# A stream encoder of two layers: one memory block a round, a later norm transposition, and engine times by intervals in the scheduling guard

## The chip, the cores and the metric

The kernel runs on one core of a Trainium2 chip. The metric is the device time of one launch in microseconds; less is better. A time is the median of several runs; the profile is of one execution of its own.

## The reference

Two layers work on x (256 rows of 2048) and on a memory of 256 rows. Each layer adds a mixer (HGRN2, retention and Mamba2 heads side by side), an attention to the memory, and a gated FFN with a short convolution. Cut to what the change touches:

```
for l in range(DEPTH):                                       # DEPTH = 2
    x = x + hybrid_mixer(rmsnorm(x, norm_mix[l]), ...)       # 11 projections of h; three recurrences; w_out
    x = x + memory_cross_attention(rmsnorm(x, norm_xattn[l]),
                                   rmsnorm(mem, norm_mem[l]), wq, wkv, wo)
    x = x + conv_glu_ffn(rmsnorm(x, norm_ffn[l]), ...)       # silu(gate) * up, 5632 wide
return rmsnorm(x, norm_final)

def rmsnorm(x, w):  return x * rsqrt(mean(x * x, -1) + EPS) * w
def hybrid_mixer(...):
    proj = h @ w_in                   # split into hq hf hi hg | rq rk rv rg | z xbc dt
    hg_out  = grouped_rmsnorm(o_hg, hg_norm, 4)  * sigmoid(hg)
    ret_out = grouped_rmsnorm(o_r, ret_norm, 4)  * silu(rg)
    ssm_out = grouped_rmsnorm(y * silu(z), ssm_norm, 4)
    return concatenate([hg_out, ret_out, ssm_out]) @ w_out
def memory_cross_attention(h, mem_n, wq, wkv, wo):
    q = h @ wq;  k, v = split(mem_n @ wkv)
    return softmax(q k^T / sqrt(128)) v @ wo    # 4 heads
```

## The kernel before, in words

Everything is float32. For the matrix products each operand is split into a high part and a low part (what the high part leaves over), and three products of the parts are added up in PSUM.

**The stream.** All weights pass through PE in one fixed order, one *step* at a time; there are 895 steps, most with eight tiles of 128 columns, that is 16 matmuls. Step n uses the weight buffers wh_n and wl_n. `split_w_hi` writes `wh` on ACT from the loaded `raw`, three steps ahead; `split_w_lo` writes `wl` on DVE (raw minus wh), two steps ahead. There are five `wh`, four `wl` and five `raw`. In layer 0 the steps are, by this number: hf to 11, hq 12 to 19, hd (hi and the Mamba2 time step DT) 20 to 27, hg 28 to 35, xbc 36 to 67, z 68 to 83, rv 84 to 91, rq, rk and rg to 115, the output projection in two halves of the rows 116 to 131 and 132 to 147, then for the attention q 148 to 155, k 156 to 163, v 164 to 171, wo 172 to 179, then the FFN to 449. Layer 1 repeats this from 450 on.

**Side work.** Whatever is not a step (evacuations, norms, the recurrences, the split of the memory) is written as a Python generator that yields after a small piece; one piece is a *round*. After each step the loop calls `advance(False)`, which gives each generator a round. Those marked `first` (evacuations) always get it; the others only while the modelled backlog of DVE and that of ACT are at most BACKLOG. The backlog is what `Metered` counts for the instructions so far, by a rate and a fixed part for each, less the length of the steps (`step_done`). So the order of the instructions is set when the program is written out, and PE, DVE and ACT then run their lists in that order.

When a step needs something that is not yet in the lists (`need`), or a projection bank while all five are taken (`pj`), all generators are advanced, whatever the backlog, until it is there. Such a burst of DVE and ACT instructions then stands right ahead of the matmul that waits for it:

```
def advance(all_of_them=True):
    for e in list(gens):
        g, first = e
        if not (first or all_of_them) and (late["dve"] + dve.us > BACKLOG or late["act"] + act.us > BACKLOG):
            continue
        ...
def step_done(us):
    for k, e in (("dve", dve), ("act", act)):
        late[k] = max(0.0, late[k] + e.us - us)
```

**The parts that the change and the prediction touch.**

- `gen_rstd` turns a sum of squares into 1/rms: a sum over partitions on PE with ONES, Ln and Exp on ACT, and one Newton step on DVE (`newton`: two operations into `w`, one into the result). For the mixer it also turns the result R into a column form RC by small matmuls with CON (line 463), and ACT copies RC. The evacuations of hd (`hi<-pj,RC`, `DT<-pj,RC`) need RC and free the banks of hd. For the memory it does the same for RM and RMC.
- The HGRN tail: OG and SQ, two sums over heads (lines 425, 426), `VV`, Ln, Exp, Newton step, `pr` (the scaled result), a copy to `mo` on ACT, and its low part `mo<-pr,mo` on DVE. `mo` is the input of the output projection. The evacuations of the last z tiles stand behind the end of this tail.
- Mamba2's and retention's group norms (`gen_ssm_norm`, `gen_ret`) end the same way, in `pr` and `mo`; the second half of the output projection (from step 132) starts with the `mo` of the second half of the Mamba2 heads.
- `gen_res` adds the output projection to X and forms H for q (`H<-X`, `ACC<-ACC,sq`).
- `gen_mem` loads the memory in eight pairs of blocks into `ya` (two buffers, `ya<-memT` on SP), and makes `mh` for each of the 16 blocks: the high part on ACT, in layer 0 also the square on ACT, the low part `mh<-ya,PAR,mh` on DVE and, in layer 0, the sum `RM<-RM,sq`. A block takes two rounds. It starts when the pages under `mh` are free, which are those of four `mo`. Step 156 is the first that reads `mh`; it reads blocks 0 to 7, and step 157 blocks 8 to 15.

Of the kernel before, what the change touches and what calls it, by code (L numbers as in the profile page):

```python
# [11 lines left out]
P = 128  # L12
T = 256
# [115 lines left out]

GROUP_MAX = 1056  # L130
NWARM = 4
BACKLOG = 10.0


def group_steps(plan):
# [112 lines left out]
class Metered:  # L248


    def __init__(self, engine, rate, fixed, fast=()):
        self.engine, self.rate, self.fixed, self.fast, self.us = engine, rate, fixed, fast, 0.0

    def __getattr__(self, name):
        f = getattr(self.engine, name)
        if name == "preload_act_table_set":
            def g(*a):
                self.us += 1.28
                return f(*a)
            return g  # L260

        def g(out, *a, **k):
            n = 1
            for d in out.shape[1:]:
                n *= d
            self.us += (n / (2 if name in self.fast else 1) + self.fixed) / self.rate
            return f(out, *a, **k)  # L267
        return g


def build(tc, ws, xT, memT, par, con, masks, rot, dec, outT):
    nc = tc.nc
    act, dve, pe, gp = Metered(nc.scalar, 1200.0, 190), Metered(nc.vector, 960.0, 64, ("tensor_scalar",)), nc.tensor, nc.gpsimd

    pc = tc.alloc_tile_pool(name="const", bufs=1)
    pw = tc.alloc_tile_pool(name="weights", bufs=1)
# [31 lines left out]
    def pcol(l, key, i, n=1):  # L308
        return parcol(l * PLAYER + PCOL[key] + i, n)
# [54 lines left out]
    def wait(*keys):  # L364
        while any(k not in flags for k in keys):
            yield
# [23 lines left out]
    def fn(out, src, f, **kw):  # L390

        want = "natural_log_exp_and_others" if f in (AF.Exp, AF.Ln) else "silu_and_others" if f in (AF.Silu, AF.Tanh) else table[0]
        if want != table[0]:
            act.preload_act_table_set(want)
            table[0] = want
        act.activation(out, src, f, **kw)
# [31 lines left out]
    def gen_rstd(acc_key, acc, out, outc, key):  # L428
        yield from wait(acc_key)
        yield  # L430
        while lock.get("v"):
            yield
        lock["v"] = 1
        yield from take(1)
        if rest:
            ps = bank()
            for i, t in enumerate([acc] + rest):
                pe.matmul(ps[:, :T], ones, t, start=i == 0, stop=i == len(rest))  # L438
        else:
            while lock.get("sq", 0) == 2:  # L440
                yield
            lock["sq"] = lock.get("sq", 0) + 1
            hl = tmp("v", [P, T], F32R, bufs=1), tmp("sq", [P, T], F32R, bufs=2)
            split_ones(acc, *hl)
            yield
            yield
            ps = bank()
            sum_ones(ps[:, :T], *hl)
            lock["sq"] -= 1
        yield  # L450
        v = tmp("v", [P, T], bufs=1)
        dve.tensor_scalar(v, ps[:, :T], 1.0 / D, EPS, ALU.mult, ALU.add)
        give()
        yield
        yield from newton(v, out)
        lock["v"] = 0
        flags.add(key)
        if outc is not None:
            yield
            yield from take(1)  # L460
            ps = bank()
            for i in range(2):
                pe.matmul(ps[:, i:i + 1], out[:, i * P:(i + 1) * P], ident[:, 0:1], start=True, stop=True)
            yield
            act.copy(outc, ps[:, 0:2])
            give()
            flags.add(key + ("c",))
# [85 lines left out]
    def layer(l):  # L553
# [479 lines left out]
        def gen_ret(p):  # L1033
# [42 lines left out]

            OG, SQ, VV = q[:, b0:b0 + 2, :], k[:, b0:b0 + 2, :], A0[:, b0:b0 + 2, :]
            yield from gen_o(pg["rv"], lambda a: ((0, A0[:, a, :], 0, True, False), (1, A1[:, a, :], P, False, True)), lambda ps: fn(SQ, ps, AF.Square), lambda ps: act.copy(OG, ps), p)
            yield from gen_gstd(SQ, P, VV, SQ)
            G = pg["rg"]  # L1080
            for i in range(2):
# [10 lines left out]

        MH = {}

        MHP = [2, 3, 6, 10, 12, 13, 14, 15]

        def gen_mem():

            yield from wait((A, "mo", 5), (A, "mo", 7), (A, "mo", 13), (A, "mo", 15))
            raw = {}  # L1100

            def fetch(p):
                if p < KD // 2:
                    raw[p] = tmp("ya", [P, 2, T])
                    nc.sync.dma_start(raw[p], memT[:, 2 * p:2 * p + 2, :])
            fetch(0)
            fetch(1)
            for _ in range(4):
                yield
            for p in range(KD // 2):  # L1110
                t = page(MHP[p], [P, 2, 2 * T], F32R, "mh")
                for b in range(2):
                    kt = 2 * p + b
                    MH[kt] = t[:, b, :]
                    split_hl(MH[kt], raw[p][:, b, :], pcol(l, "norm_mem", kt))
                    if l == 0:
                        while lock.get("sq", 0) == 2:
                            yield
                        lock["sq"] = lock.get("sq", 0) + 1
                        sq = RM if kt == 0 else tmp("sq", [P, T], bufs=2)  # L1120
                        fn(sq, raw[p][:, b, :], AF.Square)
                    yield
                    split_lo(MH[kt], raw[p][:, b, :], pcol(l, "norm_mem", kt))
                    if l == 0:
                        if kt:
                            tt(RM, RM, sq, ALU.add)
                        lock["sq"] -= 1
                    flags.add((C, "m", kt))
                    yield
                fetch(p + 2)  # L1130
            flags.add("accm")

        def qk_evac(name, pgi, r, rkey, i):
# [273 lines left out]
    with tc.manual_schedule():  # L1407
# [58 lines left out]
        for j, st in enumerate(steps):  # L1466
            if j == 0 or st["l"] != steps[j - 1]["l"]:
                for k, f in layer(st["l"]).items():
                    begins[(st["l"], k)] = f
            if 2 <= j + 2 < SINGLE + (KD - SINGLE) // 2:  # L1470
                first_h(j + 2)
            split_w_hi(j + 3)
            split_w_lo(j + 2)
            for ev, ps in done:
                start(ev(ps), True)
            done.clear()
            matmuls(st)
            if j == SINGLE:
                start(gen_first())
            if j == 5:  # L1480
                fn(ONES, one, AF.Copy)
                nc.sync.dma_start(CON, con)
            if j == 7:
                nc.sync.dma_start(PAR[:, 0:PLAYER - KD], par[:, KD + T:PLAYER + T])
            if j == 11:
                nc.sync.dma_start(PAR[:, PLAYER - KD:], par[:, PLAYER + T:])
                mf = page(16, [P, 7, 64], F32, "mf")
                nc.sync.dma_start(mf, masks)
                gp.tensor_copy(MSK, mf)
            if j == 15:  # L1490
                start(gen_lb())
            advance(False)
            step_done(st["n"] / P * 0.325)
        for ev, ps in done:
            start(ev(ps))
        start(gen_rstd((("Z",), "acc"), ACC, R, None, ("RZ",)))
# [36 lines left out]
```

## Time and profile before

| | before |
|---|---|
| median of 3 runs | 2571.71 us (2571.24 to 2572.49) |
| the profiled execution | 2571.2 us |
| its span | 2569.0 us (2.2 us lie around it) |
| mean granted clock | 0.996 |
| PE busy | 2541.8 us, 99% |
| weight load busy | 2252.0 us, 88% |
| DVE busy | 1944.6 us, 76% |
| ACT busy | 1469.1 us, 57% |

The time of a run is that of the whole launch; the span is from the first to the last instruction in the trace. A timeline row gives the start, the length and the operation, and in brackets how long the engine was idle ahead of it and whose result ended that. On DVE and ACT a row's length overlaps the start of the next row, so from start to start is the shorter measure. All side operations carry the line of one helper, 267, for both DVE and ACT, so they are told apart by their tiles.

### The profile page before, as it was taken

The numbers are of one execution on the slowest core, as the hardware profiler recorded it, in microseconds if no ns is written. First come the engines' busy times: TensorE is split into PE (matmuls) and PEld (weight loads), VectorE is DVE, ScalarE is ACT, GpSimd is POOL, SyncE is SP. The second block draws the span as 40 slices with busy tenths as digits, with TensorE's granted clock in tenths as the row PEclk, the third lists the DMA queues.
The fourth block names the chain that finished last, engine by engine and source line by source line (L and its number), as shares of the span: only waits on it lengthen the run. The fifth ranks groups of instructions, "written<-read, shape, count | busy, mean of one in ns | idle before, by whom it ended". The sixth has DMA issues, their size and how long they took to land. (4 is left out here: it accounts for less than half of the span.)

```text
span 2569.0 us, 40307 instructions
## 1 busy us (share of the span) xinstructions
PE 2541.8 (99%) x15456; PEld 2252.0 (88%) x15456; DVE 1944.6 (76%) x3093; ACT 1469.1 (57%) x2155; POOL 5.3 (0%) x12
## 2 busy tenths in 40 slices
PE   9999999999999999999999999999999999999998
PEld 8888988898888888888898888889988888888887
DVE  6798699778776567776678888996787765677765
ACT  6667575566555345555567755665665543555543
POOL 0000000000000000000000000000000000000000
PEclk9999999999999999999999999999999999999999
DMA  7456656545656666665665576565666656666654
GB/s 273 154 169 194 200 170 199 193 156 189 190 188 191 186 197 190 188 191 185 191 193 168 157 229 189 178 207 182 182 189 190 193 181 193 193 189 191 192 183 130
DMA packets 141392, 482.02 MB, mean 188 GB/s; under 512 B 15312, under 2 KB 21648, under 8 KB 141200
## 3 DMA queue, kind: packets, MB, share of 16 engines
q1 hardware_dynamic: 140912, 479.17, 59.8%
q8 instruction: 122, 2.00, 0.3%
q14 instruction: 70, 0.57, 0.1%
q10 hardware_dynamic: 288, 0.27, 0.0%
HBM read 477.25 MB, written 2.13 MB: 187 GB/s over the span
## 5 line engine op out<-in xcount | busy, mean ns | idle before, releaser
L1380 PE MATMUL pj<-H,wh 128*128 128x512 f32 x4480 | 1562.0, 393 | 3.0 <-DVE hg L267 2.5
L267 DVE TENSOR_TENSOR wl<-raw,wh 128x1024 fp32r<-128x1024 f32 (+2 forms) x895 | 1076.1, 1205 | 416.4 <-PE pj L1381 216.3
L267 ACT ACTIVATE wh<-raw 128x1024 fp32r<-128x1024 f32 (+2 forms) x895 | 931.8, 1046 | 618.5 <-PE pj L1380 336.7
L1381 PE MATMUL pj<-H,wl 128*128 128x256 f32 x4480 | 1253.9, 280 | 3.2 <-DVE wl L267 3.1
L1380 PEld LDWEIGHTS pj<-H,wh 128*128 128x128 f32 x4480 | 841.8, 188 | 189.6 <-DVE hg L267 2.6
L1381 PEld LDWEIGHTS pj<-H,wl 128*128 128x128 f32 x4480 | 842.0, 188 | 5.9 <-DVE wl L267 5.2
L1380 PE MATMUL pj<-g,wh 128*128 128x512 f32 x1386 | 480.7, 392 | 0.0
L1381 PE MATMUL pj<-g,wl 128*128 128x256 f32 x1386 | 387.4, 280 | 0.0
L1380 PEld LDWEIGHTS pj<-g,wh 128*128 128x128 f32 x1386 | 260.1, 188 | 57.5
L1381 PEld LDWEIGHTS pj<-g,wl 128*128 128x128 f32 x1386 | 260.1, 188 | 0.0
L267 ACT COPY e<-pj 128x256 f32<-128x256 f32 x288 | 106.2, 370 | 233.3 <-PE pj L1381 228.3
L1380 PE MATMUL pj<-mo,wh 128*128 128x512 f32 x512 | 178.4, 392 | 1.3 <-DVE mo L267 0.9
L267 DVE SCALAR_TENSOR_TENSOR ya<-UPAD,PAR,ya 128x256 f32<-128x256 f32 x352 | 146.4, 479 | 0.0
L1381 PE MATMUL pj<-mo,wl 128*128 128x256 f32 x512 | 143.2, 280 | 1.2 <-DVE wl L267 1.2
L267 DVE TENSOR_TENSOR X<-X,pj 128x256 f32<-128x256 f32 x215 | 90.0, 420 | 70.7 <-PE pj L1381 59.8
L1380 PEld LDWEIGHTS pj<-mo,wh 128*128 128x128 f32 x512 | 96.1, 188 | 23.3 <-DVE mo L267 1.2
L1381 PEld LDWEIGHTS pj<-mo,wl 128*128 128x128 f32 x512 | 96.1, 188 | 1.6 <-DVE wl L267 1.5
L267 ACT ACTIVATE ya<-UPAD,PAR 128x256 f32<-128x256 f32 x176 | 94.7, 588 | 2.2 <-DVE g L267 2.2
L267 DVE TENSOR_TENSOR UPAD<-pj,e 128x256 f32<-128x256 f32 x208 | 86.7, 419 | 0.2
L267 DVE TENSOR_TENSOR UPAD<-UPAD,R 128x512 f32<-128x512 f32 (+1 forms) x120 | 74.3, 621 | 4.0
L1401 PE MATMUL pj<-wh,H 128*128 128x264 f32 (+1 forms) x256 | 72.8, 284 | 0.0
L1403 PE MATMUL pj<-wh,H 128*128 128x264 f32 (+1 forms) x256 | 72.4, 283 | 0.0
(283 smaller groups left out, 1971.2 us busy)
## 6 DMA issues: line engine op xcount, KB each, us to landing
raw<-ws SPq DMA_DIRECT2D x777, 512.0 KB, 4.0
raw<-ws SPq DMA_DIRECT2D x96, 448.0 KB, 3.4
raw<-ws SPq DMA_DIRECT2D x16, 528.0 KB, 4.1
DE<-CD SPq DMA_DIRECT2D x8, 512.0 KB, 5.1
ya<-memT SPq DMA_DIRECT2D x16, 256.0 KB, 4.2
DS<-CD SPq DMA_DIRECT2D x8, 256.0 KB, 5.6
raw<-ws SPq DMA_DIRECT2D x6, 256.0 KB, 4.2
outT<-y SPq DMA_DIRECT2D x3, 512.0 KB, 2.9
```

The source lines that it names most:

```text
L267: return f(out, *a, **k)
L1380: pe.matmul(ps, wh[:, a], s, start=first, stop=False)
L1381: pe.matmul(ps[:, :T], wl[:, a], s[:, :T], start=False, stop=last)
L1401: pe.matmul(ps, xh, wh[:, a], start=f, stop=False)
L1403: pe.matmul(ps, xl, wh[:, a], start=False, stop=e)
```

## The change

Four things are changed. The limit BACKLOG is 5.6 instead of 10. `Metered` counts by other figures: on ACT a fixed part of 130 instead of 190 cycles, on DVE 68 instead of 64, no halving for tensor_scalar, 40 more for scalar_tensor_tensor and 140 more for copy_predicated; a step counts 0.347 us for 128 columns, not 0.325, so that 5.6 is two steps of eight tiles. `gen_rstd` has one round more ahead of the matmuls of RC and RMC. And `gen_mem` waits for two `mo` and for the second half of retention, and for the two other `mo` only at pair 4; the pages are taken in another order; it starts three rounds after its first loads, not four, and makes the high part of one block and the low part of the block before in the same round.

```
-BACKLOG = 10.0
+BACKLOG = 5.6
...
-            self.us += (n / (2 if name in self.fast else 1) + self.fixed) / self.rate
+            self.us += (n + self.fixed + self.more.get(name, 0)) / self.rate
...
-    act, dve, pe, gp = Metered(nc.scalar, 1200.0, 190), Metered(nc.vector, 960.0, 64, ("tensor_scalar",)), nc.tensor, nc.gpsimd
+    act, dve, pe, gp = Metered(nc.scalar, 1200.0, 130), Metered(nc.vector, 960.0, 68, {"scalar_tensor_tensor": 40, "copy_predicated": 140}), nc.tensor, nc.gpsimd
...
         if outc is not None:
+            yield
             yield
             yield from take(1)
...
+            flags.add((A, "ret", p))
             yield from gen_gstd(SQ, P, VV, SQ)
...
-        MHP = [2, 3, 6, 10, 12, 13, 14, 15]
+        MHP = [2, 3, 10, 12, 6, 13, 14, 15]
...
-            yield from wait((A, "mo", 5), (A, "mo", 7), (A, "mo", 13), (A, "mo", 15))
+
+            yield from wait((A, "mo", 13), (A, "mo", 15), (A, "ret", 1))
...
-            for _ in range(4):
-                yield
-            for p in range(KD // 2):
-                t = page(MHP[p], [P, 2, 2 * T], F32R, "mh")
-                for b in range(2):
-                    kt = 2 * p + b
-                    MH[kt] = t[:, b, :]
-                    split_hl(MH[kt], raw[p][:, b, :], pcol(l, "norm_mem", kt))
...
-                    yield
-                    split_lo(MH[kt], raw[p][:, b, :], pcol(l, "norm_mem", kt))
...
-                    yield
-                fetch(p + 2)
+            for _ in range(3):
+                yield
+
+            def low(kt):
+                p, b = kt // 2, kt % 2
+                split_lo(MH[kt], raw[p][:, b, :], pcol(l, "norm_mem", kt))
...
+                flags.add((C, "m", kt))
+                if b:
+                    fetch(p + 2)
+            sqs = {}
+            for kt in range(KD):
+                p, b = kt // 2, kt % 2
+                if not b:
+                    if p == 4:
+                        yield from wait((A, "mo", 5), (A, "mo", 7))
+                    t = page(MHP[p], [P, 2, 2 * T], F32R, "mh")
+                    MH[kt], MH[kt + 1] = t[:, 0, :], t[:, 1, :]
+                split_hl(MH[kt], raw[p][:, b, :], pcol(l, "norm_mem", kt))
...
+                if kt:
+                    low(kt - 1)
+                yield
+            low(KD - 1)
...
-            step_done(st["n"] / P * 0.325)
+            step_done(st["n"] / P * 0.347)
```

Every instruction of PE and DVE is still there, and ACT has four table loads more. What changes is the order, at three places above all.

DVE ahead of step 84, before. `w`, `RR` and `VV` are the HGRN tail's Newton step, `pr` and `mo` its result, `z1` the z sum whose bank step 84 takes.

```order
L267 SCALAR_TENSOR_TENSOR pr_5_2607<-OG_1_2313,HGW_108,RR_1_2315 128x256 x2
L267 SCALAR_TENSOR_TENSOR w_3_2610<-RR_1_2315 128x512
L267 TENSOR_TENSOR w_3_2610<-w_3_2610,VV_1_2314 128x512
L267 TENSOR_TENSOR wl_83_2615<-raw_83_2476,wh_83_2583 128x1024
L267 SCALAR_TENSOR_TENSOR RR_1_2315<-w_3_2610,RR_1_2315 128x512
L267 TENSOR_TENSOR wl_84_2639<-raw_84_2502,wh_84_2613 128x1024
L267 TENSOR_TENSOR mo_1_2606<-pr_5_2607,mo_1_2606 128x2x256
L267 SCALAR_TENSOR_TENSOR pr_6_2662<-OG_1_2313,HGW_108,RR_1_2315 128x256 x2
L267 TENSOR_TENSOR wl_85_2667<-raw_85_2532,wh_85_2637 128x1024
L267 TENSOR_TENSOR wl_86_2690<-raw_86_2561,wh_86_2665 128x1024
L267 TENSOR_TENSOR mo_2_2661<-pr_6_2662,mo_2_2661 128x2x256
L267 TENSOR_TENSOR z1_1_2696<-pj_37_2478,e_33_2697 128x256
```

The same stretch after, right behind wl_86.

```order
L267 SCALAR_TENSOR_TENSOR w_2_2677<-RR_1_2472 128x512
L267 TENSOR_TENSOR w_2_2677<-w_2_2677,VV_1_2471 128x512
L267 TENSOR_SCALAR VV_1_2471<-ms_15_2667 128x512
L267 SCALAR_TENSOR_TENSOR RR_1_2472<-w_2_2677,RR_1_2472 128x512
L267 SCALAR_TENSOR_TENSOR pr_5_2685<-OG_1_2470,HGW_108,RR_1_2472 128x256 x2
L267 SCALAR_TENSOR_TENSOR w_3_2688<-RR_1_2472 128x512
L267 TENSOR_TENSOR w_3_2688<-w_3_2688,VV_1_2471 128x512
L267 SCALAR_TENSOR_TENSOR RR_1_2472<-w_3_2688,RR_1_2472 128x512
L267 TENSOR_TENSOR mo_1_2684<-pr_5_2685,mo_1_2684 128x2x256
L267 SCALAR_TENSOR_TENSOR pr_6_2695<-OG_1_2470,HGW_108,RR_1_2472 128x256 x2
L267 TENSOR_TENSOR mo_2_2694<-pr_6_2695,mo_2_2694 128x2x256
L267 TENSOR_TENSOR z1_1_2700<-pj_37_2450,e_33_2701 128x256
```

The wl of the steps 83 to 86, which stood between the operations of the tail, now stand ahead of it, and the tail is one piece from the second `VV` to the z sum.

DVE ahead of step 132, before. `zsq` is the scale of the Mamba2 group norm, `mo_5` what step 132 reads, `X` the sums of the output projection.

```order
L267 TENSOR_TENSOR wl_130_4158<-raw_130_4015,wh_130_4129 128x1024
L267 TENSOR_TENSOR X2_84<-X2_84,pj_68_4135 128x256 x2
L267 SCALAR_TENSOR_TENSOR w_11_4181<-zsq_2_3896 128x512
L267 TENSOR_TENSOR w_11_4181<-w_11_4181,zsq_2_3896 128x512
L267 SCALAR_TENSOR_TENSOR zsq_2_3896<-w_11_4181,zsq_2_3896 128x2x256
L267 SCALAR_TENSOR_TENSOR pr_17_4186<-xbc1_1_1611,PAR_78,zsq_2_3896 128x256 x2
L267 TENSOR_TENSOR wl_131_4191<-raw_131_4045,wh_131_4156 128x1024
L267 TENSOR_TENSOR X3_85<-X3_85,pj_69_4162 128x256 x2
L267 SCALAR_TENSOR_TENSOR pr_18_4216<-xbc1_1_1611,PAR_78,zsq_2_3896 128x256 x2
L267 TENSOR_TENSOR wl_132_4221<-raw_132_4073,wh_132_4189 128x1024
L267 TENSOR_TENSOR X3_85<-X3_85,pj_70_4195 128x256 x2
L267 TENSOR_TENSOR mo_5_4185<-pr_17_4186,mo_5_4185 128x2x256
```

After, the last twelve operations up to the same `mo_5`; `rk` and `rq` belong to retention's norm.

```order
L267 TENSOR_TENSOR X3_85<-X3_85,pj_72_4222 128x256 x2
L267 SCALAR_TENSOR_TENSOR w_10_4259<-rk_1_3193 128x512
L267 TENSOR_TENSOR w_10_4259<-w_10_4259,rA0_1_2715 128x512
L267 SCALAR_TENSOR_TENSOR rk_1_3193<-w_10_4259,rk_1_3193 128x512
L267 TENSOR_TENSOR rq_1_3082<-rq_1_3082,rg_1_3565 128x256 x2
L267 TENSOR_SCALAR zsq_2_4131<-ms_37_4256 128x2x256
L267 SCALAR_TENSOR_TENSOR w_11_4268<-zsq_2_4131 128x512
L267 TENSOR_TENSOR w_11_4268<-w_11_4268,zsq_2_4131 128x512
L267 SCALAR_TENSOR_TENSOR zsq_2_4131<-w_11_4268,zsq_2_4131 128x2x256
L267 SCALAR_TENSOR_TENSOR pr_17_4273<-xbc1_1_1608,PAR_78,zsq_2_4131 128x256 x2
L267 SCALAR_TENSOR_TENSOR pr_18_4278<-xbc1_1_1608,PAR_78,zsq_2_4131 128x256 x2
L267 TENSOR_TENSOR mo_5_4272<-pr_17_4273,mo_5_4272 128x2x256
```

The Newton step of `zsq`, which had wl_131 and wl_132 behind it, now stands in one run between the X of step 131 and `mo_5`; the Newton step of retention's norm is ahead of it in the same run.

DVE in the second half of the output projection, before: `mh` and `RM` are the memory's.

```order
L267 TENSOR_TENSOR X2_84<-X2_84,pj_81_4520 128x256 x2
L267 SCALAR_TENSOR_TENSOR mh_1_4478<-ya_3_4356,PAR_78,mh_1_4478 128x256
L267 TENSOR_TENSOR wl_144_4580<-raw_144_4417,wh_144_4547 128x1024
L267 SCALAR_TENSOR_TENSOR H7_93<-X1_83,PAR_78,H7_93 128x256
L267 TENSOR_TENSOR ACC_104<-ACC_104,sq_23_4573 128x256
L267 TENSOR_TENSOR X2_84<-X2_84,pj_82_4553 128x256 x2
L267 TENSOR_TENSOR wl_145_4613<-raw_145_4449,wh_145_4578 128x1024
L267 SCALAR_TENSOR_TENSOR H8_94<-X2_84,PAR_78,H8_94 128x256
L267 TENSOR_TENSOR ACC_104<-ACC_104,sq_24_4604 128x256
L267 TENSOR_TENSOR X2_84<-X2_84,pj_83_4584 128x256 x2
L267 SCALAR_TENSOR_TENSOR mh_1_4478<-ya_3_4356,PAR_78,mh_1_4478 128x256
L267 TENSOR_TENSOR RM_103<-RM_103,sq_25_4609 128x256
```

After, from the same X on.

```order
L267 TENSOR_TENSOR X2_84<-X2_84,pj_81_4522 128x256 x2
L267 TENSOR_TENSOR wl_144_4580<-raw_144_4421,wh_144_4548 128x1024
L267 SCALAR_TENSOR_TENSOR H7_93<-X1_83,PAR_78,H7_93 128x256
L267 TENSOR_TENSOR ACC_104<-ACC_104,sq_23_4574 128x256
L267 TENSOR_TENSOR X2_84<-X2_84,pj_82_4554 128x256 x2
L267 TENSOR_TENSOR wl_145_4610<-raw_145_4453,wh_145_4578 128x1024
L267 SCALAR_TENSOR_TENSOR H8_94<-X2_84,PAR_78,H8_94 128x256
L267 TENSOR_TENSOR ACC_104<-ACC_104,sq_24_4604 128x256
L267 TENSOR_TENSOR X2_84<-X2_84,pj_83_4584 128x256 x2
L267 TENSOR_TENSOR wl_146_4640<-raw_146_4486,wh_146_4608 128x1024
```

There is no `mh` between these any more. The first `mh` of DVE now stands behind wl_154 and the next behind wl_157; before they stand behind wl_143, 145, 147, 149, 152, 154 and 156.

## Rows read from the trace of the kernel before

**Rows 1.** The page, part 1: engine, busy us, share of span, instructions.

```profile
PE 2541.8 (99%) x15456; PEld 2252.0 (88%) x15456; DVE 1944.6 (76%) x3093; ACT 1469.1 (57%) x2155; POOL 5.3 (0%) x12
```


**Rows 2.** Waits of PE: engine, line, waited-for; us in total, times, longest us.

```profile
PE pj L1380 <- DVE mh L267: 4.5, 2, 2.5
PE pj L1381 <- DVE wl L267: 4.2, 4, 1.3
PE pj L1380 <- DVE hg L267: 2.5, 1, 2.5
...
PE pj L1380 <- DVE mo L267: 0.9, 1, 0.9
```


**Rows 3.** Busy us by stretch: PE, PEld, DVE, ACT, POOL; clock, DMA, GB/s.

```profile
84.50:87.70 3.20, 3.20 (x10) 2.72 (x11) 2.35 (x6) 2.79 (x5) 0.00 (x0) 0.52 0.00 0
425.00:452.00 27.00, 27.00 (x157) 23.76 (x156) 26.69 (x56) 19.27 (x38) 0.00 (x0) 1.00 0.51 180
472.50:486.00 13.50, 8.63 (x35) 5.82 (x34) 11.43 (x28) 8.25 (x19) 0.00 (x0) 0.80 0.40 133
```


**Rows 4.** Timeline of PE (start, length), behind step 29 and at step 84.

```profile
81.36 0.61 PE L463 MATMUL ms<-CON,R 128*128 128x1 f32 x4
...
250.96 0.37 PE L1401 MATMUL pj<-wh,H 128*128 128x256 f32 x1
```


**Rows 5.** Timeline of ACT around step 30.

```profile
85.26 0.14 ACT L267 COPY RC<-ms 128x2 f32<-128x2 f32 x1
...
90.90 0.46 ACT L267 ACTIVATE hi<-pj,RC 128x256 f32<-128x256 f32 x1
91.26 0.26 ACT L267 ACTIVATE DT<-pj,RC 128x8 f32<-128x8 f32 x1
```


**Rows 6.** Timeline of DVE ahead of step 84.

```profile
249.40 0.42 DVE L267 TENSOR_TENSOR z<-pj,e 128x256 f32<-128x256 f32 x1
```


**Rows 7.** Timeline of DVE, 384 to 413 us.

```profile
388.04 0.75 DVE L267 TENSOR_TENSOR rq<-rq,rg 128x256 f32<-128x256 f32 x2
...
390.63 0.68 DVE L267 TENSOR_SCALAR zsq<-ms 128x512 f32<-128x512 f32 x1
...
394.28 0.87 DVE L267 TENSOR_TENSOR X<-X,pj 128x256 f32<-128x256 f32 x2
395.07 0.68 DVE L267 SCALAR_TENSOR_TENSOR w<-zsq 128x512 f32<-128x512 f32 x1
395.79 0.69 DVE L267 TENSOR_TENSOR w<-w,zsq 128x512 f32<-128x512 f32 x1
396.52 0.69 DVE L267 SCALAR_TENSOR_TENSOR zsq<-w,zsq 128x512 f32<-128x512 f32 x1
397.24 0.88 DVE L267 SCALAR_TENSOR_TENSOR pr<-xbc,PAR,zsq 128x256 f32<-128x256 f32 x2
...
402.68 0.68 DVE L267 TENSOR_TENSOR mo<-pr,mo 128x512 fp32r<-128x512 f32 x1
```


**Rows 8.** Timeline of ACT, 384 to 413 us.

```profile
391.35 1.30 ACT L267 ACTIVATE zsq<-zsq 128x512 f32<-128x512 f32 x2 [2.73 <-DVE zsq L267]
...
406.71 0.63 ACT L267 ACTIVATE mo<-pr 128x512 fp32r<-128x512 f32 x1 [3.31 <-DVE pr L267]
```


**Rows 9.** Timeline of DVE, 340 to 376 us.

```profile
348.77 0.28 DVE L267 TENSOR_SCALAR DE<-DE,CUM 128x128 f32<-128x128 f32 x1
...
350.93 0.29 DVE L267 TENSOR_SCALAR DS<-DS,CUM 128x128 f32<-128x128 f32 x1
...
358.12 1.22 DVE L267 TENSOR_TENSOR DE<-DE,DS 128x1024 f32<-128x1024 f32 x1
```


**Rows 10.** Issues of the ya loads on SP: last line of that view.

```profile
DMA to landing us min/median/max: 3.1/4.6/8.0
```


**Rows 11.** Timeline of ACT at the values, 505 to 540 us.

```profile
517.76 0.84 ACT L267 ACTIVATE v<-pj,RMC 128x256 f32<-128x256 f32 x2 [4.09 <-PE pj L1403]
```

More of the change, by code (lines that the diff above doesn't have):

```diff
@@ L248, with __init__ @@
 class Metered:
-    def __init__(self, engine, rate, fixed, fast=()):
-        self.engine, self.rate, self.fixed, self.fast, self.us = engine, rate, fixed, fast, 0.0
+    def __init__(self, engine, rate, fixed, more={}):
+        self.engine, self.rate, self.fixed, self.more, self.us = engine, rate, fixed, more, 0.0
     def __getattr__(self, name):
@@ L1107, in gen_mem @@
             fetch(1)
-            for _ in range(4):
+            for _ in range(3):
                 yield
-            for p in range(KD // 2):
-                t = page(MHP[p], [P, 2, 2 * T], F32R, "mh")
-                for b in range(2):
-                    kt = 2 * p + b
-                    MH[kt] = t[:, b, :]
-                    split_hl(MH[kt], raw[p][:, b, :], pcol(l, "norm_mem", kt))
-                    if l == 0:
-                        while lock.get("sq", 0) == 2:
-                            yield
-                        lock["sq"] = lock.get("sq", 0) + 1
-                        sq = RM if kt == 0 else tmp("sq", [P, T], bufs=2)
-                        fn(sq, raw[p][:, b, :], AF.Square)
-                    yield
-                    split_lo(MH[kt], raw[p][:, b, :], pcol(l, "norm_mem", kt))
[L1124 to L1128, printed above, removed]
-                    yield
-                fetch(p + 2)
+            def low(kt):
+                p, b = kt // 2, kt % 2
+                split_lo(MH[kt], raw[p][:, b, :], pcol(l, "norm_mem", kt))
+                if l == 0:
+                    if kt:
+                        tt(RM, RM, sqs.pop(kt), ALU.add)
+                    lock["sq"] -= 1
+                flags.add((C, "m", kt))
[10 more added lines that the diff above has]
+                split_hl(MH[kt], raw[p][:, b, :], pcol(l, "norm_mem", kt))
+                if l == 0:
+                    while lock.get("sq", 0) == 2:
+                        yield
+                    lock["sq"] = lock.get("sq", 0) + 1
+                    sqs[kt] = RM if kt == 0 else tmp("sq", [P, T], bufs=2)
+                    fn(sqs[kt], raw[p][:, b, :], AF.Square)
+                if kt:
+                    low(kt - 1)
+                yield
+            low(KD - 1)
             flags.add("accm")
```

## The prediction

> **What bounds the kernel now.** I read the page first: PE is busy 99% of the span and its weight load 88% [rows 1], so the kernel is a stream of weight steps on PE, and what can be won or lost is where PE stands still. The waits of PE [rows 2] hold nearly all of that: for the memory's `mh` 4.5 us, for `wl` 4.2 in four waits, for `hg` 2.5, for `mo` 0.9. The table by stretches [rows 3] shows what such a wait is made of. In 425 to 452 us PE is busy throughout: 157 matmuls in 27.00 us, 0.172 us each and 2.75 us for a step of 16. DVE is busy 26.69 of these 27 us, so in this stretch DVE has nothing to spare, whatever its mean over the span. In 472.5 to 486 us, which are the two steps 156 and 157 (the first on the memory), PE is busy 8.63 of 13.50 us: two full steps would be 5.50, so 8.0 us are lost there. In 84.50 to 87.70 us, right behind the wait for `hg`, the granted clock is 0.52, which is the 1.2 GHz level, and ten matmuls take 3.20 instead of 1.72 us: about 1.5 us on top of a wait of 2.5 us.
>
> **The sum is made against the profiled run**, 2571.2 us (span 2569.0 and 2.2 around it); the median of the runs, 2571.71, is 0.5 away and makes no difference. Instruction counts stay the same on PE and DVE, and ACT gets four table loads more; so the change pays or costs only by order. I took from the order of both kernels what stands ahead of each matmul that waits for another engine, and priced these chains with rows. A step is named by its `wl`: step 84 uses wl_84.
>
> **What goes away.** The lower limit spreads side work thinner, and in the order no `wl` stands behind a long run any more at steps 60, 116 and 514. I take the waits for `wl` and the one for `mo` as gone, 4.2 + 0.9 = 5.1 [rows 2], and about 1 for smaller ones and for what PE needs to pick up again: a gain of 6, between 4.5 and 7.
>
> **Step 32 (two more rounds before RC).** The matmuls that turn R into RC move from behind step 29, where they lie in the wait for `hg`, to behind step 31. Step 32 needs a bank that a `DT`/`hi` evacuation frees, and that needs RC. The matmuls 0.61 [rows 4], the copy 0.14, `hi` 0.46 and `DT` 0.26 [rows 5] now stand alone: 1.5 us, between 0.5 and 2. The wait for `hg` ahead of step 30 stays, since the same normalisations of `hf` and `hq` are ahead of it.
>
> **Step 84 (first matmuls of rv).** They want two of five projection banks, of which z holds four until the HGRN output is done. In before that is at 249.40, the first z sum [rows 6], and step 84 starts at 250.96 [rows 4]: 1.5 us of slack. In after the sums over heads are behind steps 81 and 83 instead of 75 and 77, so everything after the second sum is in one run on DVE ahead of the z sum: VV (a tensor-scalar of 512, 0.68), Ln and Exp on ACT (1.30 [rows 8]), a Newton step of three operations (0.72 + 0.73 + 0.72 = 2.17 start to start), a `mo` subtraction 0.68, two `pr` 0.88 [rows 7], the `mo` copy on ACT 0.63 [rows 8], the second `mo` 0.68, the z sum 0.42 [rows 6]. Together 7.4 us. PE covers about 1.0 of it (four transposes and three matmuls), so 6.4 us are lost, and 1.5 for the clock as after `hg` [rows 3]: 7.9, between 5.5 and 9. Nothing else hides it: the next instruction of PE is the waiting one.
>
> **Steps 118 and 119.** Ahead of the two `mo` that these steps read, DVE now has in one run twelve scalings of 128 columns (twelve rows from 348.77 to 350.93 [rows 9], 2.35), a Newton step 2.17, two `rq` 0.75 [rows 7], four small sums (two like the z sum, two of 128 columns) 1.4, DE times DS 1.22 [rows 9], two `mo` 1.4 and three `wl`, of the same shape as DE times DS, 3.7: 13.0 us against three steps of PE, 8.25. These durations overlap by some 0.1 at each of 25 operations, and DVE may enter a little ahead; I take 3, between 0 and 4.5.
>
> **Step 132 (second half of the output projection).** Before, the sum for the group norm of z is behind step 122 and its Newton step at 395.07 [rows 7], so only 0.9 is waited for `mo` [rows 2]. In after the second sum is behind step 131 itself, and ahead of the `mo` that step 132 reads stand, from the end of step 131 on: two X 0.87, the Newton step of rk 2.17, two `rq` 0.75, zsq 0.68, Ln and Exp 1.30 [rows 8], a Newton step 2.17, four `pr` 1.76, `mo` 0.68 [rows 7]: 10.4 us. The sum's matmuls cover half a microsecond. 9.8 and 1.5 for the clock: 11.3, between 8 and 13. This is the largest term.
>
> **Steps 156 and 157 (the memory split).** The new split needs one round for a block where the old needs two, but it may advance only while the modelled backlog is under two steps. Through steps 139 to 152 the duties of DVE alone fill a step (26.69 of 27 us in before [rows 3], with one block every second step in it), so the guard holds it. In the order, before has the low parts of seven blocks behind wl_143, 145, 147, 149, 152, 154 and 156, and nine are left when step 156 asks; after has two, behind wl_154 and wl_157, and 14 left. These are forced out in one burst, for which there are two `ya` buffers: a pair's work of about 1.5 us and then its next transfer, at the least 3.1 us to landing [rows 10], for two pairs in turn, so 2.3 us a pair. Five blocks more are 2.5 pairs: 5.8 us on top of the 8.0 lost before. If transfers land ahead, 3; with the median landing of 4.6 us [rows 10], 7.6.
>
> A rule speaks for this part: the Trainium skill, "Perfetto Trace Analysis", Optimizing Scalar/DVE Operations, says that where Scalar and Vector are not saturated but cause bubbles elsewhere, work broken into smaller pieces may complete sooner. By it the memory's wait would go, and the whole sum would come to about 2584. The condition does not hold here by the row of 425 to 452 us, where DVE is saturated; so I keep 5.8.
>
> **End of step 171.** The memory's norm is ready four steps later (sum behind step 165, not 161), so both last heads' scores, 16 transposes and the products with v fall behind one step, where ACT still has four `v` evacuations (0.84 for two [rows 11]) and four exponentials of the same 256 columns. No row shows this burst, hence wide bounds, 0 and 6; I take the sum of the eight, 3.4, less a little overlap: 3.
>
> **The FFN and layer 1.** In layer 1 the memory has no squares to add, so its backlog is small; beyond the gain above I expect nothing. The FFN's order is the same. The four table loads lie on ACT, outside the chains above, and are taken at nothing; inside one each would cost what a table load takes there, about what Ln and Exp take together, 1.3 us [rows 8].
>
> **Sum.** Losses 1.5 + 7.9 + 3 + 11.3 + 5.8 + 3 = 32.5, gain 6: +26.5, so 2571.2 + 26.5, about 2597 (it would be +10 with all low ends and a gain of 7, +38 with all high ends and a gain of 4.5).
>
> **Rivals.** (a) The other side, faster: the change does what it says. If step 84's and 132's chains start early enough to be covered, the gain of 6 stays and an evenly spread memory split takes back the 8.0: 2571 - 14 = 2557. It decides at the sums' matmuls: these would have to stand three steps (8.25 us) earlier than the order has them. Against it: the order is fixed, and 7.4 and 10.4 us of work stand between them and the matmul that waits. (b) Only the two long chains bind; the memory's burst costs what it costs now, and steps 118 and 171 wait for nothing: 1.5 + 7.9 + 11.3 - 6 = +15, 2586. For it: DVE is idle for 2 of the 13.50 us of 472.5 to 486 [rows 3], and transfers may land at their minimum. (c) No change, since PE is busy 99% and nothing is done to its work: 2571. Against it: the 8.0 us in the row of 472.5 to 486 us show that order alone costs time. (d) Worse: behind stops of 6 to 10 us the slow clock lasts longer than after 2.5, or DVE enters a burst late from the one before: five more microseconds in each of two or three places, 2608 to 2620.
>
> For (c) a page speaks too: the Trainium skill, "Perfetto Trace Analysis", Identifying the Most-Contended Engine, wants the engine with the highest occupancy worked on first and TensorE judged by its weight-load share. By it the order on the other engines would not matter. The trace agrees with the 88% over the span, and shows DVE at 99% in one stretch, so I give that little weight.
>
> **How the numbers follow.** Forecast 0.62, with its own range 2588 to 2608; (b) 0.20, (d) 0.08, (a) 0.06, (c) 0.04. The range 2580 to 2608 takes in the forecast, most of (b) and the bounds of the priced waits. A measurement tells about 0.2%, 5 us, from no change: faster 0.06, same 0.04, slower 0.90.
>
> **What would show it.** In after, PE should show waits of about 6 us for `z` near 253 us and of about 9 for `mo` near 420, two `mh` waits of more than 4.5 us in all, and none for `wl` over 1 us; DVE should have no `mh` row before step 153. If the first two are missing, the chains are covered and the forecast is wrong by most of its size; if only `mh` or the end of step 171 differs, by one term.

## The result, and the profile after

The changed kernel takes 2607.85 us (median of 4 runs, 2604.67 to 2609.45) against 2572.1 us: the ratio is 1.0138, with a 95% interval of 1.0126 to 1.0150. It is slower by 36 us; the prediction was 2597, with a range to 2608, so the time lies 0.15 us inside the upper end. The profiled run has a span of 2602.8 us, 33.8 more than before.

The waits of PE in the changed kernel answer to [rows 2] (engine, line, waited-for; us in total, times, longest; the change shifts the line numbers by about 12):

```profile
PE pj L1392 <- DVE mo L267: 13.6, 3, 9.7
PE pj L1392 <- DVE mh L267: 6.8, 4, 3.3
PE pj L1413 <- DVE z L267: 6.6, 1, 6.6
PE pj L1393 <- DVE wl L267: 3.0, 4, 1.5
PE pj L1392 <- DVE hg L267: 3.0, 1, 3.0
```

The waits for `mo` have gone from 0.9 to 13.6 us, the one for `z` is new, those for `mh` have grown by half, and the waits for `wl`, which were to go, are still 3.0 us.

Where the time went shows best by stretches that begin and end with the first matmul of the same step in both kernels. The table by stretches of the changed kernel (busy us of PE, PEld, DVE, ACT, POOL; granted clock, DMA share, GB/s):

```profile
85.02:96.38 11.36, 10.45 (x52) 9.12 (x53) 8.35 (x18) 10.84 (x20) 0.00 (x0) 0.87 0.33 92
96.38:250.76 154.38, 154.12 (x1045) 135.63 (x1043) 135.40 (x214) 106.70 (x141) 0.57 (x1) 1.00 0.54 172
250.76:262.41 11.65, 5.07 (x28) 4.87 (x26) 10.71 (x21) 6.99 (x11) 0.00 (x0) 0.71 0.48 167
262.41:383.97 121.56, 115.37 (x726) 102.07 (x725) 93.46 (x168) 70.19 (x94) 0.00 (x0) 0.99 0.56 178
...
416.64:436.82 20.18, 10.45 (x52) 8.79 (x50) 17.03 (x30) 8.38 (x12) 0.00 (x0) 0.75 0.40 126
...
498.07:519.95 21.88, 14.88 (x50) 10.07 (x49) 17.30 (x41) 13.73 (x33) 0.00 (x0) 0.69 0.41 133
519.95:568.34 48.39, 45.97 (x325) 42.30 (x323) 27.23 (x48) 23.84 (x46) 0.95 (x1) 1.00 0.47 152
```

And of the kernel before, for step 84, steps 131 to 133 and steps 156 to 158:

```profile
250.96:254.22 3.26, 3.26 (x32) 3.26 (x30) 3.19 (x8) 2.96 (x3) 0.00 (x0) 1.00 0.95 323
...
401.81:411.18 9.37, 8.49 (x50) 7.22 (x48) 9.27 (x18) 4.93 (x7) 0.00 (x0) 1.00 0.56 177
...
472.54:489.41 16.87, 12.00 (x51) 8.74 (x49) 13.76 (x31) 9.89 (x22) 0.00 (x0) 0.80 0.42 136
```

| steps | before, us | after, us | difference | the prediction's term |
|---|---|---|---|---|
| 30 to 32 | 10.00 | 11.36 | +1.4 | 1.5 |
| 33 to 83 | 156.46 | 154.38 | -2.1 | in the gain of 6 |
| 84 | 3.26 | 11.65 | +8.4 | 7.9 |
| 85 to 119 | 115.73 | 121.56 | +5.8 | 3, with a part of the gain |
| 120 to 130 | 31.86 | 32.67 | +0.8 | |
| 131 to 133 | 9.37 | 20.18 | +10.8 | 11.3 |
| 134 to 155 | 61.36 | 61.25 | -0.1 | |
| 156 to 158 | 16.87 | 21.88 | +5.0 | 5.8 |
| 159 to 171 | 44.86 | 48.39 | +3.5 | 3 |

The other lengths of before are from the same view of its trace, from step to step as in the table. With +0.5 ahead of step 30 and -0.3 behind step 171, the FFN and layer 1 included, these make the 33.8 us.

The two long chains are the predicted ones. The timeline of DVE in the changed kernel (start, length), from the first result of the HGRN tail to the z sum:

```profile
251.84 0.88 DVE L267 SCALAR_TENSOR_TENSOR pr<-OG,HGW,RR 128x256 f32<-128x256 f32 x2
252.63 0.68 DVE L267 SCALAR_TENSOR_TENSOR w<-RR 128x512 f32<-128x512 f32 x1
...
254.69 0.68 DVE L267 TENSOR_TENSOR mo<-pr,mo 128x512 fp32r<-128x512 f32 x1
255.29 0.88 DVE L267 SCALAR_TENSOR_TENSOR pr<-OG,HGW,RR 128x256 f32<-128x256 f32 x2
256.86 0.69 DVE L267 TENSOR_TENSOR mo<-pr,mo 128x512 fp32r<-128x512 f32 x1 [0.69 <-ACT mo L267]
257.47 0.42 DVE L267 TENSOR_TENSOR z<-pj,e 128x256 f32<-128x256 f32 x1
```

The timeline of PE in the same place, with the matmul that waits and in brackets for how long and for what:

```profile
257.94 0.58 PE L1413 MATMUL pj<-wh,H 128*128 128x256 f32 x1 [6.58 <-DVE z L267]
```

And the timeline of DVE ahead of the second half of the output projection:

```profile
419.63 0.88 DVE L267 TENSOR_TENSOR X<-X,pj 128x256 f32<-128x256 f32 x2
420.43 0.68 DVE L267 SCALAR_TENSOR_TENSOR w<-rk 128x512 f32<-128x512 f32 x1
...
423.15 0.69 DVE L267 TENSOR_SCALAR zsq<-ms 128x512 f32<-128x512 f32 x1
425.19 0.69 DVE L267 SCALAR_TENSOR_TENSOR w<-zsq 128x512 f32<-128x512 f32 x1 [1.36 <-ACT zsq L267]
...
427.37 1.67 DVE L267 SCALAR_TENSOR_TENSOR pr<-xbc,PAR,zsq 128x256 f32<-128x256 f32 x4
428.95 0.69 DVE L267 TENSOR_TENSOR mo<-pr,mo 128x512 fp32r<-128x512 f32 x1
```

The matmul of step 132 that waits for it, in the timeline of PE:

```profile
429.79 0.76 PE L1392 MATMUL pj<-mo,wh 128*128 128x512 f32 x1 [9.73 <-DVE mo L267]
```

No `wl` stands between these operations any more: in each chain DVE goes from one to the next and stops only for ACT, 0.69 us for the copy to `mo` and 1.36 for Ln and Exp, and PE has nothing else to do. PE waits 6.58 us, where the prediction had 6.4, and 9.73, where it had 9.8.

### The profile page after: what moved, and what is told of

Its sections match the earlier page's. It is cut to its first block, busy times and chain, and to the rows that moved or that the text cites. A ratio compares the mean times of both kernels' runs of the same rounds, so it can differ in the third digit from the quotient of the medians.

```text
span 2602.8 us, 40328 instructions
## 1 busy us (share of the span) xinstructions
PE 2550.4 (98%) x15456; PEld 2258.0 (87%) x15456; DVE 1947.5 (75%) x3093; ACT 1477.9 (57%) x2159; POOL 5.7 (0%) x12
## 4 chain that ended last, share of the span: by engine, by line
PE 94%; DVE 3%; ACT 1%; DMA 1%; issue 0%; DVEq 0%; ACTq 0%
PE pj L1392 56%; PE pj L1393 28%; PE pj L1413 2%; PE pj L1415 2%; PE pj L1414 2%; DVE wl L267 1%; PE pj L1396 1%; PE pj L1397 1%; PE pj L1395 1%; DMA DS<-CD 0%; DVE w L267 0%; PE ms L711 0%; PE ms L809 0%; PE ms L976 0%; ACT wh L267 0%
## 5 line engine op out<-in xcount | busy, mean ns | idle before, releaser
L1392 PE MATMUL pj<-mo,wh 128*128 128x512 f32 x512 | 181.3, 397 | 13.6 <-DVE mo L267 13.6
L1413 PE MATMUL pj<-wh,H 128*128 128x264 f32 (+1 forms) x256 | 73.8, 288 | 6.6 <-DVE z L267 6.6
```

The lines of the kernel that those rows point to most:

```text
L1392: pe.matmul(ps, wh[:, a], s, start=first, stop=False)
L1413: pe.matmul(ps, xh, wh[:, a], start=f, stop=False)
```

## The experiments

All compare with the kernel before on the same chip; three chips were used, and the kernel before takes 2571.7 to 2571.8 us on each, so that runs can be set side by side too. Theory G says that the guard's low limit puts the side chains behind their dates; its rival N, that the rewritten split and the later round are what cost. Theory L came up when the order of the changed kernel with the memory exempt from the guard was laid beside its code: the new split takes a square buffer for a block while the square of the block before is not yet added, so it needs two; there are two, and the residual's norm holds one at each step from 139 to 152.

**1 and 2. The guard taken back, and the guard alone.** The first is the changed kernel with `Metered`, the limit and the step length of before; the second the kernel before with only these changed.

```
-BACKLOG = 5.6                                  # the first, against the changed kernel
+BACKLOG = 10.0
-    act, dve, ... = Metered(nc.scalar, 1200.0, 130), Metered(nc.vector, 960.0, 68, {...}), ...
+    act, dve, ... = Metered(nc.scalar, 1200.0, 190), Metered(nc.vector, 960.0, 64, ("tensor_scalar",)), ...
-            step_done(st["n"] / P * 0.347)
+            step_done(st["n"] / P * 0.325)
```

The second has the same lines the other way round, against the kernel before.

> The changed kernel with the guard of before (limit 10, the old costs and 0.325 a column group); the one more round ahead of RC and the new memory split stay. Theory G (the guard's low limit puts the side chains behind their dates): the waits at step 84 (6.6 us for z) and ahead of step 132 (9.7 for mo) go, as do the long steps 118 and 171; what stays is about 1.4 us at step 31 and a burst for the memory of 12 to 14 us lost in steps 156 and 157 instead of 8.0, so 2577 to 2583 us. Theory N (the rewritten memory split and the later round cost most of it): over 2595.

> The kernel before with the new guard alone (limit 5.6, new costs, 0.347); memory split and RC round as in before. Theory G: the waits at step 84, step 118 and step 132 come back at the sizes of the changed kernel, within 1 us each, and the burst for the memory with 15 of 16 blocks left; 2600 to 2608 us, without the 1.4 us at step 31. Theory N: under 2585.

With the old guard 2577.4 us, ratio 1.0022 (1.0013 to 1.0032). The guard alone: 2611.65 us, ratio 1.0154 (1.0133 to 1.0174). The waits of PE with the old guard:

```profile
PE pj L1392 <- DVE mh L267: 8.3, 5, 2.8
...
PE pj L1392 <- DVE mo L267: 0.9, 1, 0.9
```

The waits of PE with the guard alone:

```profile
PE pj L1380 <- DVE mo L267: 14.0, 3, 9.7
PE pj L1380 <- DVE mh L267: 11.3, 7, 3.6
PE pj L1401 <- DVE z L267: 6.6, 1, 6.6
...
PE pj L1380 <- ACT DT L267: 2.2, 1, 2.2
```

Theory G holds: with the guard come the waits for z (6.6 us in both) and `mo` (9.7 the longest in both), without it they go. N falls as the main cause; the 5.7 us that are left in the first run are the split and the round. The guard alone is 4 us above what was expected and slower than the whole change: in its trace steps 156 and 157 take 22.9 us where the change has 18.2, and steps 159 to 171 take 51.0 instead of 48.4. The split doesn't pay for that by itself: run 9 below, with the new split but without the round, is no faster (2613.8 us).

**3. The limit or the prices.** The changed kernel with the limit 10 and all else as changed, the new costs too.

```
-BACKLOG = 5.6
+BACKLOG = 10.0
```

> The changed kernel with the limit 10 instead of 5.6, all else as changed, the new costs too. If the limit is the cause: the waits at steps 84 and 132 go, the burst for the memory stays (13 of 16 blocks left), 2575 to 2581 us, as with the whole old guard. If the truer costs are the cause: over 2590.

2576.8 us, ratio 1.0019 (1.0009 to 1.0030): the same as with the whole old guard. So with the new costs it is the step from 10 to 5.6 that costs about 31 us; at the limit 10 the truer costs change nothing that can be measured. The low limit with the old costs wasn't run.

**4 and 5. What holds the memory split.** First the split exempt from the guard, then also with the low part ahead of the next square, so that it never holds two square buffers:

```
-            start(gen_mem())
+            start(gen_mem(), True)          # 4 and 5: a round whatever the backlog
...
                 split_hl(MH[kt], raw[p][:, b, :], pcol(l, "norm_mem", kt))
+                if kt:                      # 5 only
+                    low(kt - 1)
                 if l == 0:
                     while lock.get("sq", 0) == 2:
                         yield
                     ...
-                if kt:
-                    low(kt - 1)
                 yield
```

> The changed kernel, but the memory split gets its round whatever the backlog. Theory G as the prediction told it (the guard holds the split): the 16 blocks are done ahead of step 156, the 13 us lost in steps 156 to 158 go, 2592 to 2596 us. Theory L (the split is held by its own lock: it wants the second of two square buffers while it still holds one, and the residual's norm holds the other at each of the steps 139 to 152): three blocks get through, the others are forced as before, 12 to 13 us are still lost in steps 156 to 158, 2604 to 2608.

> As the run before, and the low part of the block before now stands ahead of the next block's square, so that the split never holds two square buffers. Theory L: one block a step from step 137 on, the 13 us in steps 156 to 158 go, 2592 to 2597 us. Rival D (DVE has nothing to spare there, 26.69 of 27 us in before): the blocks push wl or X back, PE waits in steps 140 to 152 instead, for wl or H, by 5 us or more in all: over 2598.

2602.0 and 2601.8 us, the first 2 us under its range, the second 5 over that of theory L. In the order of the first, the low parts stand behind wl_137, 138 and 139, and then none until wl_156. Its waits of PE for `mh` are those of the changed kernel:

```profile
PE pj L1392 <- DVE mh L267: 6.6, 5, 2.5
```

In the second there are none for `mh`, but waits of PE for `X`:

```profile
PE pj L1392 <- DVE X L267: 3.1, 2, 2.4
```

And its table by stretches has, for steps 148 and 149 and for steps 156 to 158:

```profile
479.18:489.94 10.76, 7.62 (x34) 6.17 (x33) 10.66 (x24) 7.87 (x16) 0.00 (x0) 0.84 0.51 171
506.58:514.90 8.32, 8.32 (x50) 7.32 (x49) 5.77 (x9) 4.14 (x6) 0.00 (x0) 1.00 0.64 189
```

Theory L holds: without the guard, but with the lock, nothing is won in steps 156 to 158 (21.6 us for 21.9; what this trace is shorter lies mostly at step 171, 10.1 for 12.4), and without both they take 8.3. Rival D (DVE has no room there) holds for the time: with one block a step from wl_137 to wl_152 DVE falls behind, and PE pays 5.2 us in steps 148 and 149; steps 159 to 171 took 2.6 more.

**6 and 7. The split alone, mended.** The kernel before with the new split and the lines above in their new order; in the second run it is exempt from the guard too.

> The kernel before with the new memory split, mended: the low part of the block before stands ahead of the next block's square, so the split holds one square buffer only; guard and RC round as in before. In the order the 16 low parts then stand behind wl_139 to wl_159, with 2 of them left for the burst at step 156, not 9. Theory L: the 8.0 us lost in steps 156 and 157 shrink to under 3, and DVE, which idles little from 425 to 452 us, gives some back in waits for X or wl in steps 140 to 152: 2564 to 2568 us. Rival D (DVE has no room, so all comes back): 2570 to 2574.

> As the run before, with the memory split exempt from the guard as well: one block a step behind wl_138 to wl_153, none left at step 156. Theory L alone: the whole 8.0 us go, 2563. Rival D: 0.74 us of DVE a step on top of some 2.5 duties against steps of 2.77 make DVE late by about half a microsecond a step, X falls behind and PE waits for it around steps 148 and 149 as in the unlocked run of the changed kernel (5 us there, where DVE came in late): 2566 to 2571, no better than the guarded one.

Guarded: 2561.8 us, ratio 0.9962 (0.9947 to 0.9976). Exempt: 2568.9, ratio 0.9988 (0.9978 to 0.9997). The guarded one beats both kernels, by 10 us and by 46, and lies 2 us under what was expected. The table by stretches of the guarded run, for 425 to 452 us and for steps 156 to 158:

```profile
425.00:452.00 27.00, 27.00 (x157) 23.77 (x156) 26.73 (x55) 19.66 (x37) 0.00 (x0) 1.00 0.63 202
473.28:481.83 8.55, 8.55 (x52) 7.55 (x51) 8.48 (x18) 6.85 (x14) 0.00 (x0) 1.00 0.68 228
```

And of the exempt run, for 425 to 452 us and for steps 148 and 149:

```profile
425.00:452.00 27.00, 27.00 (x158) 23.76 (x157) 26.73 (x57) 20.20 (x40) 0.00 (x0) 1.00 0.60 199
450.86:461.30 10.44, 7.64 (x35) 6.21 (x34) 10.34 (x23) 7.76 (x16) 0.00 (x0) 0.84 0.51 176
```

Steps 156 to 158 take 8.55 us, a full pace, for 16.87 before. In both runs DVE is busy 26.73 of 27 us from 425 to 452; the guarded one leaves PE unharmed, the other makes it wait 2.8 us for `X`. In the order, the exempt run has a block behind each `wl` from wl_138 to wl_153; the guarded one has none behind wl_147 to wl_150, just ahead of where the other pays. So a guard has its use here, at 10.

**8. HGRN exempt.** The changed kernel with HGRN's rounds whatever the backlog.

```
-            start(gen_hgrn())
+            start(gen_hgrn(), True)
```

> The changed kernel, but the HGRN chain gets its round whatever the backlog. Theory G: its sums stand behind steps 75 and 77 again, the wait of 6.6 us for z at step 84 goes with its slow clock (8.4 in the step), the rest stays: 2597 to 2601 us if nothing else is pushed back, and no lower than 2593. Rival: what HGRN takes early, the others lose, so that the wait only moves to steps 113 to 132: 2604 to 2608.

2583.3 us, ratio 1.0044 (1.0028 to 1.0060): 24 us less, where at most 15 was expected. The wait for z goes (step 84 takes 3.3 us), and with it most of those of the chains behind it; its waits of PE for `mo`, and the one for `hg`, which is paid twice now:

```profile
PE pj L1392 <- DVE hg L267: 6.1, 2, 3.1
...
PE pj L1392 <- DVE mo L267: 3.2, 2, 2.9
```

The longest wait for `mo` is 2.9 for 9.7, and step 113 takes 2.8 us for 8.2. Both expectations were wrong. In the trace, the scale of the second Mamba2 norm starts behind wl_129, not wl_134. One late chain had made the next ones late; through which of the things that they share (banks, the work buffers, the backlog itself) wasn't tried.

**9. One round before RC.** The changed kernel without the added round in `gen_rstd`.

```
         if outc is not None:
             yield
-            yield
             yield from take(1)
```

> The changed kernel without the one more round ahead of the matmuls of RC and RMC; the order of DVE's chains is the same. The prediction's step 32: 1.4 us less between the starts of steps 30 and 33 (11.4 in the changed kernel), 2603 to 2608 us in all. Rival: with the low limit the RC chain is late anyway, as in the run with the guard alone, where these three steps took 12.5: no gain, or 1 us more.

2613.8 us, ratio 1.0162 (1.0142 to 1.0182). The table by stretches, for step 171 and for steps 30 to 32:

```profile
561.82:578.94 17.12, 12.29 (x59) 9.91 (x57) 7.29 (x22) 7.50 (x25) 0.95 (x1) 0.70 0.11 32
84.82:97.29 12.47, 10.26 (x48) 8.65 (x49) 8.31 (x14) 11.97 (x22) 0.00 (x0) 0.86 0.29 84
```

The changed kernel itself takes 2609.65 us on this chip (run 10), so leaving the round out costs 4 us. Steps 30 to 32 take 12.47 us without the round and 11.36 with it, and 12.47 too with the guard alone: under the low limit the round costs nothing there. With the limit 10 it costs something, 10.9 us in the traces of runs 3 and 11 and 11.5 in that of run 1, for 10.0 without it. What is late without the round isn't RC. The timeline of ACT in this run has its copy long ahead of the first `hi`:

```profile
86.53 0.14 ACT L267 COPY RC<-ms 128x2 f32<-128x2 f32 x1
...
92.18 0.45 ACT L267 ACTIVATE hi<-pj,RC 128x256 f32<-128x256 f32 x1
```

Between the two ACT loads a table and works on `hf` and a `wh`. In before they stand at 85.26 and 90.90 [rows 5]; here `hi` comes 1.3 us later and PE earlier, since step 30 takes 2.88 us for 4.45. PE waits 2.2 us for `DT`, and step 32 then takes 4.45 us for 2.77, at a clock of 0.62 for 1.00. Step 171 takes 17.12 us here for 12.42, part of it at a granted clock of 0.70 for 1.00. That this is the missing round isn't shown: it takes 16.4 in run 5 too, which has the round.

**10. The changed kernel again**, without any edit.

> The changed kernel once more, for a second trace: the same waits for z (6.6), mo (9.7 the longest) and mh. Its times so far lie 4.8 us apart, the kernel before's 2 to 3. If the slow clock behind a wait differs from run to run, the steps behind the four long waits differ by up to 1.5 us each between the two traces while the waits for z and mo stay within 0.1; if not, all steps agree within 0.3 us.

2609.65 us (2607.3 to 2612.0); the span of its trace is 2610.1, 7.3 more than the first. Its waits of PE are those of the first trace but for `mh`, 0.3 more, `H`, 0.5 more, and `wl`, 1.2 more:

```profile
PE pj L1392 <- DVE mo L267: 13.6, 3, 9.7
...
PE pj L1413 <- DVE z L267: 6.6, 1, 6.6
PE pj L1393 <- DVE wl L267: 4.2, 5, 2.2
```

The step behind the wait of 9.7 us, step 132, in the first trace (table by stretches; the clock is the last but two):

```profile
429.79:434.05 4.26, 4.26 (x17) 3.68 (x18) 3.17 (x6) 0.86 (x1) 0.00 (x0) 0.64 0.49 155
```

And in the second trace:

```profile
435.01:440.27 5.26, 5.25 (x16) 4.49 (x17) 3.18 (x6) 0.86 (x1) 0.00 (x0) 0.50 0.57 195
```

The same 16 matmuls take 4.26 us at a mean clock of 0.64, or 5.26 at 0.50: in the second trace the whole step ran at 1.2 GHz. The steps 7, 30, 112, 113, 132 and 158 differ by 0.6 to 1.5 us, by the clock or by a longer wait for `wl`, and they hold 5.6 of the 7.3.

**11 and 12. The rest of the change, mended, and a higher limit.** The changed kernel with the limit 10 and the lines of 5 in their new order; and the guarded kernel of 6 with the limit 12.

```
-BACKLOG = 5.6                                  # 11, with the new order of low(kt - 1)
+BACKLOG = 10.0
...
-BACKLOG = 10.0                                 # 12, against run 6
+BACKLOG = 12.0
```

> The changed kernel with its two suspected faults taken out, all else as changed: limit 10 instead of 5.6, and the low part of the block before ahead of the next block's square. In the order the memory's blocks stand behind wl_138 to wl_155, none is left for step 156. Theories G and L: no wait over 3 us for z, mo or mh; the 13 us lost in steps 156 to 158 go, and some of it comes back in waits for X, 2 to 5 us, since the split runs one block a step as in the unguarded run: 2563 to 2569 us. If either theory lacks a part: over 2572.

> The kernel before with the mended memory split and the limit 12 instead of 10. The blocks stand behind wl_136 to wl_156, the chains of HGRN and Mamba2 one or two steps earlier than in before. Theory G read the other way: nothing waited for these chains any more at 10, so earlier buys nothing, and wl may wait behind longer runs of DVE: 2560 to 2566 us. Rival: a higher limit goes on paying: under 2559.

2565.15 us, ratio 0.9973 (0.9964 to 0.9983), and 2564.3, ratio 0.9970 (0.9959 to 0.9981). Both times are as expected; of the waits for `X` in the first, 2 to 5 us were expected and 1.6 came. The first shows that limit and lock are the change's two faults: without them it is faster than the kernel before. The second shows that a higher limit buys nothing more; its longest wait of PE is new, 3.5 us for a tile of retention (`rA`).


## Why the prediction was right, and where it was not

**Direction and mechanism** hold, by runs 1 to 3 and 11: order alone costs the time, by bursts right ahead of the matmul that waits, and the largest terms are steps 84 and 132. Of the rivals, (a) and (c) fell. (b) had the two chains right, but the burst and step 171 bind as well. What (d) feared, a slow clock that lasts longer behind long waits, is in the second trace of the changed kernel, a microsecond a place; the time lies at the lower end of (d)'s range.

**Step 84** (8.4 for 7.9) **and step 132** (10.8 for 11.3): the chains were priced from rows of before, one operation after the other, and came out within half a microsecond, slow clock included.

**The gain of 6** is the term that was mis-sized most. Steps 33 to 83 won 2.1 us. The waits that were named did go, at steps 60, 116 and 514. The fourth of the four, 1.04 us at step 7, was counted as gone without a reason and is still there. And the low limit makes new runs ahead of other `wl`; the longest is at step 113:

```profile
351.84 0.38 PE L1393 MATMUL pj<-H,wl 128*128 128x256 f32 x1 [1.49 <-DVE wl L267]
```

The step that failed is to have looked only at the old places for what the new order does to `wl`, and to have taken all four waits as gone.

**Steps 118 and 119.** The wait ahead of step 118 is 3.2 us, as priced (3); with the one of 0.7 at step 119 it is two of the three for `mo`. But steps 85 to 119 together lose 5.8: the wait for `wl` above, 0.9 for `DS` right behind it, and 1.1 us more of busy PE in these steps (115.4 for 114.3) were not in the sum.

**Steps 156 to 158** (5.0 for 5.8): size right, reason half right. The guard does hold the split, until wl_154; but without the guard the lock holds it, and the prediction did not see the lock. That the burst goes at the pace of the `ya` loads fits the trace: in it ACT waits for them three times, 4.9 us, and in before once, 2.4. That DVE has nothing to spare, which was read from 26.69 of 27 us, fits runs 5 and 7, where one block a step makes PE wait for `X`. It isn't the whole truth: run 6 puts the 16 blocks behind wl_139 to wl_159 and PE loses nothing, with the same busy share. A busy share near 1 doesn't tell how far an engine is ahead of its dates. The sentence of the Trainium skill on smaller pieces ("Perfetto Trace Analysis", Optimizing Scalar/DVE Operations), which the prediction set aside, is about breaking up instructions, and no run here shows it: the `mh` operations of DVE are 32 of 128x256 in before, in after and in run 6. What takes steps 156 to 158 from 16.87 to 8.55 us in run 6 is their earlier place in the list.

**Step 32** (1.4 for 1.5): size and path right. The timelines of PE and ACT in the changed kernel have the chain that was priced, from the matmuls with CON behind step 31 to the first matmul of step 32, 1.41 us later:

```profile
92.08 0.50 PE L464 MATMUL ms<-CON,R 128*128 128x1 f32 x4
...
92.81 0.47 ACT L267 ACTIVATE hi<-pj,RC 128x256 f32<-128x256 f32 x1
...
93.49 0.50 PE L1392 MATMUL pj<-H,wh 128*128 128x512 f32 x1 [0.91 <-ACT DT L267]
```

But it isn't the price of the round alone: by runs 2 and 9 the low limit costs 2.5 us here without it, by another path.

**Step 171** (3.5 for 3): within its wide bounds.

**The signs.** The waits for `z` and `mo` came as said. The waits for `mh` were four, not two (6.8 us), two for `wl` are over 1 us (steps 7 and 113), and the first `mh` of DVE comes at 485.4 us, in PE's step 151: it stands behind wl_154, which is made two steps ahead.

**What is left** of the distance, 2597 to 2607.85. About 7 us of it are in the first trace, and nearly all of these in the gain and steps 118 and 119: the other five terms come out at 29.1 us for 29.5, and everything else in the table adds up to +4.6, where the prediction had 3 - 6. The other 3 are that the traced run, 2604.67 us, is the fastest of the four; the second trace is 7.3 us longer, with nearly the same waits, and in part by the clock. That the time still fell inside the range is luck: two of the four runs (2609.34 and 2609.45) and the median of run 10 (2609.65) lie above 2608.

## What to carry to other kernels

A limit on modelled backlog is a trade: too low, it defers work that has a date, and the work comes back as one uncovered chain right ahead of the reader; look for the chain's last producer and count what stands behind it in the list, not at mean busy shares. Chains late by a few steps can make the next ones late, so exempting the first of them can pay more than its own wait (24 us for 8.4 in run 8). When a generator is rewritten to overlap two pieces, count how many of each shared buffer it now holds at once: here, with the limit left at 10, one call placed earlier turned a loss of 5 us (run 3) into a gain of 6.5 (run 11).

## What was not expected of the hardware

The clock behind a wait isn't the same from run to run. Behind the same wait of 9.7 us the same step took 4.26 us at a mean granted clock of 0.64 in one trace and 5.26 at 0.50 in another, and behind the same wait of 2.5 us for `hg` step 30 took 4.45 us at 0.62 in before and 2.90 at 1.00 in run 6. The times of a kernel spread too: 2604.67 to 2612.0 for the changed kernel over its six runs, 2561.3 to 2563.3 for the best one over five. That the clock behind waits makes this spread isn't shown: run 7 has none of the long waits and spreads from 2565.6 to 2570.0.
